# One-core decoder trunk: the first MLP product as seven block products, with weight sums in buffers of their own

## The chip, the cores and the metric

One NeuronCore of a Trainium2 chip runs the whole program. The time is the device time of one execution in microseconds (us); lower is better. TensorE (PE) multiplies, VectorE (DVE) and ScalarE (ACT) do elementwise work, GpSimd (POOL) issues the accumulating DMAs of this kernel, and SyncE (SP) issues the plain ones.

## The reference

A trunk of four layers over 512 tokens of 1024 features. Each layer adds a token mixer (sliding-window attention, a Conformer convolution, an HGRN2 recurrence, attention again) and then a squared-ReLU MLP with 4096 hidden features:

```python
def squared_relu_mlp(h, w1, w2):
    return jnp.square(jax.nn.relu(h @ w1)) @ w2
...
        h = h + y
        h = h + squared_relu_mlp(rms_norm(h, norm_mlp[i]), mlp_w1[i], mlp_w2[i])
    return rms_norm(h, final_norm)
```

All is float32. The factor of the norm is taken out of the MLP: the squared ReLU lets it be applied, squared, to the result (`r2`, `nr2`).

## The kernel before

**Precision.** Every operand is held as two float32r parts, high and low, and a product is three matmuls: high by high, high by low, low by high (lines 279 to 287). The high part is an ACT cast, the low part a DVE subtraction (`load`, line 262, for weights; line 557 and 558 for activations).

**Weights.** A plan lists all blocks of weights in the order of use, 512 KB each. `load` takes the next: a DMA into a `raw` tile on SP's queue, then the cast and the subtraction into a pair of tiles `wh`, `wl`, of which there are five (`W_BUFS`). `prefetch` runs it up to five blocks ahead of those that PE has finished (`n_done`), as the code is written out; each engine then works through its own list in order.

**The MLP** goes in four groups of 1024 hidden features a layer, 16 in all. The first product of a group is plain (`linear`): eight output tiles of 128 features, each 8 x 3 matmuls with 512 tokens as moving columns. The second product, 512 x 1024 by 1024 x 1024 in 2 x 2 blocks, is done with seven block products instead of eight (`PRODUCTS`). Each takes a block or a combination of blocks of the hidden activations U (s1 to s4) and of the weights W (t1 to t4):

```python
    ("U11 W11", "x", ((0, 0, 1),)),
    ("U12 W21", "z", ((0, 0, 1),)),
    ("s1 t1", "y", ((1, 1, -1),)),
    ("s2 t2", "x", ((0, 1, -1),)),
    ("s4 W22", "y", ((0, 1, -1),)),
    ("s3 t3", "x", ((1, 1, -1),)),
    ("U22 t4", "x", ((1, 0, 1),)),
```

The letter names a pair of PSUM banks that goes on accumulating; after the named product a result is read out and added to `rows` (line 604). A block of weights is 512 x 512 and comes in two halves, each one block of the plan (14 a group). t1, t2 and t4 are made one after the other in the tile that held W11, each by a DMA on POOL's queue that adds another block to the tile in place (line 217); t3 is made in the tile of W12 in that way. All these tiles come from a pool of the MLP with eight buffers (line 211), so each W block of a half has its own. Blocks of the first product use another pool, `rawp`, of three.

The s operands are made by DVE and cast by ACT up to three products ahead (`operand`). The normalised rows are turned by PE transposes into `xs`, 512 tokens wide, and PE starts on them as they come (`lead`).

## Time and profile before

| | us |
|---|---|
| median of 3 runs | 2170.0 (2169.82 to 2171.41) |
| the profiled execution | 2173.1, of which the span from first to last instruction is 2171.3 |
| PE busy | 2121.1 (98%) |
| PE weight loads, beside the matmuls | 1748.1 (81%) |
| DVE busy | 1402.4 (65%) |
| ACT busy | 1156.5 (53%) |
| POOL busy | 200.5 (9%) |
| mean DMA rate | 120 GB/s |

A busy PE is not a PE at its peak: matmuls overlap, and the records show each as longer than the step from one to the next. The granted clock of PE is full in nearly all of the span. Times of rows are from the start of the span. The waits of an engine that isn't the bottleneck cost nothing; those of PE do.

### The profile page before, as it was taken

Reading aid. Unit: us, or ns where it says so; the run is one execution under the profiler, and the core shown is the slowest. Engines: PE = TensorE matmul, PEld = TensorE weight load, DVE = VectorE, ACT = ScalarE, POOL = GpSimd, SP = SyncE. Lnnn points to the kernel's source line nnn. Section 1 sums busy time; section 2 is a strip of 40 time slices with the busy share of each in tenths; the row PEclk is TensorE's granted clock in tenths of the full one; section 3 lists DMA queues with packets and bytes.
Section 4 is the critical chain, followed back from the end, with each engine's and each line's share of the span. In section 5 each row is a group of like instructions: output and inputs, shape, how many; then the busy total and the mean of one; then the engine's idle time right before and its main releaser. Section 6 shows DMA issues by size and latency. Waiting matters only on the chain.

```text
span 2171.3 us, 27234 instructions
## 1 busy us (share of the span) xinstructions
PE 2121.1 (98%) x10226; PEld 1748.1 (81%) x10226; DVE 1402.4 (65%) x2226; ACT 1156.5 (53%) x2015; POOL 200.5 (9%) x193
## 2 busy tenths in 40 slices
PE   8999999999988999999999999999999999999997
PEld 7778888888877888888788888888887878888886
DVE  6864663769986375475888874547548784637547
ACT  6855454454684445445555554534536684534534
POOL 0000110110020011011300000101100000101100
PEclk9999999999998999999999999999999999999999
DMA  5154755745214375674222226567564116557553
GB/s 152 47 155 110 181 129 152 184 68 136 69 40 136 98 184 114 168 175 88 88 62 75 78 69 179 113 164 177 118 161 88 59 50 194 120 152 188 114 125 78
DMA packets 211063, 262.56 MB, mean 121 GB/s; under 512 B 9027, under 2 KB 136003, under 8 KB 210932
## 3 DMA queue, kind: packets, MB, share of 16 engines
q1 hardware_dynamic: 175540, 191.61, 28.1%
q0 software_dynamic: 35392, 69.21, 20.1%
q8 instruction: 81, 1.33, 0.2%
q14 instruction: 50, 0.41, 0.1%
HBM read 258.69 MB, written 2.10 MB: 120 GB/s over the span
## 4 chain that ended last, share of the span: by engine, by line
PE 72%; DVE 14%; ACT 5%; DMA 5%; issue 4%; SPq 0%; DVEq 0%; ACTq 0%
PE mm L285 21%; PE mm L286 21%; PE mm L287 21%; DVE wl L262 5%; DMA raw<-in_mlp_w_dram 4%; DVE rows L604 3%; PE aux L754 2%; DVE ul L558 2%; DVE uc L893 1%; PE aux L704 1%; ACT wh L262 1%; PE aux L1068 1%; ACT uc L912 1%; PE aux L438 1%; PE aux L738 1%
## 5 line engine op out<-in xcount | busy, mean ns | idle before, releaser
L262 DVE TENSOR_TENSOR wl<-raw,wh 128x1024 fp32r<-128x1024 f32 x452 | 551.2, 1220 | 538.9 <-ACT wh L262 536.3
L262 ACT CAST wh<-raw 128x1024 fp32r<-128x1024 f32 x452 | 470.0, 1048 | 497.7 <-PE mm L286 187.9
L285 PE MATMUL mm<-x,wh 128*128 128x512 f32 x1568 | 628.9, 401 | 0.0
L286 PE MATMUL mm<-x,wh 128*128 128x512 f32 x1568 | 613.7, 391 | 0.0
L287 PE MATMUL mm<-x,wl 128*128 128x512 f32 x1568 | 613.6, 391 | 0.0
L287 PEld LDWEIGHTS mm<-x,wl 128*128 128x128 f32 x1568 | 294.6, 188 | 62.5 <-issue 1.2
L286 PEld LDWEIGHTS mm<-x,wh 128*128 128x128 f32 x1568 | 295.6, 189 | 56.6 <-issue 1.8
L285 PEld LDWEIGHTS mm<-x,wh 128*128 128x128 f32 x1568 | 295.5, 188 | 55.7 <-issue 1.1
L285 PE MATMUL mm<-wh,uh 128*128 128x512 f32 x768 | 303.1, 395 | 15.9 <-DVE rows L604 12.6
L217 POOL DMA_DIRECT2D raw<-in_mlp_w_dram x128 | 153.5, 1206 | 1773.2 <-DVE wl L262 928.4
L286 PE MATMUL mm<-wl,uh 128*128 128x512 f32 x768 | 300.0, 391 | 0.0
L287 PE MATMUL mm<-wh,ul 128*128 128x512 f32 x768 | 298.0, 391 | 0.0
L285 PEld LDWEIGHTS mm<-wh,uh 128*128 128x128 f32 x768 | 144.5, 188 | 53.8 <-issue 10.6
L287 PEld LDWEIGHTS mm<-wh,ul 128*128 128x128 f32 x768 | 144.6, 188 | 30.3
L286 PEld LDWEIGHTS mm<-wl,uh 128*128 128x128 f32 x768 | 144.8, 189 | 28.9
L563 ACT ACTIVATE relu<-mm 128x512 f32<-128x512 f32 x128 | 76.0, 594 | 166.7 <-PE mm L287 166.7
L558 DVE TENSOR_TENSOR ul<-us,uh 128x1024 fp32r<-128x1024 f32 x64 | 78.0, 1218 | 32.5 <-ACT uh L557 32.5
L604 DVE SCALAR_TENSOR_TENSOR rows<-mm,nr,rows 128x512 f32<-128x512 f32 x128 | 94.9, 741 | 0.0
L564 ACT ACTIVATE us<-relu 128x512 f32<-128x512 f32 x128 | 80.9, 632 | 3.9
L285 PE MATMUL mm<-wh,y 128*128 128x512 f32 x192 | 78.1, 407 | 1.4 <-ACT y L366 1.4
L426 ACT ACTIVATE sq<-rows 128x512 f32<-128x512 f32 x64 | 40.2, 628 | 68.3 <-DVE rows L338 54.3
L287 PE MATMUL mm<-wh,y 128*128 128x512 f32 x192 | 76.0, 399 | 0.0
(232 smaller groups left out, 2546.5 us busy)
## 6 DMA issues: line engine op xcount, KB each, us to landing
raw<-in_mlp_w_dram SPq DMA_DIRECT2D x256, 512.0 KB
raw<-in_mlp_w_dram POOLq DMA_DIRECT2D x128, 512.0 KB, 6.1
raw<-in_hgrn_w_qfig_dram SPq DMA_DIRECT2D x64, 256.0 KB
raw<-in_attn_w_qkv_dram SPq DMA_DIRECT2D x20, 512.0 KB
raw<-in_attn_w_o_dram SPq DMA_DIRECT2D x16, 512.0 KB
raw<-in_conv_w_pw_dram SPq DMA_DIRECT2D x32, 256.0 KB
raw<-in_conv_w_pw_dram SPq DMA_DIRECT2D x8, 512.0 KB
raw<-in_hgrn_w_o_dram SPq DMA_DIRECT2D x8, 512.0 KB
```

The costliest lines, as they stand in the source:

```text
L217: gp.dma_start(out=wide(to), in_=block(w, r, c, h), accum_op=ALU.add)
L262: return sc.copy(wh, raw), ve.tensor_tensor(wl, raw, wh.bitcast(F32), ALU.subtract)
L285: pe.matmul(ps, sh, mh, start=start, stop=False, skip_group_check=again)
L286: pe.matmul(ps, sh, ml, start=False, stop=False, skip_group_check=again)
L287: pe.matmul(ps, sl, mh, start=False, stop=stop, skip_group_check=again)
L426: sc.activation(scratch("sq"), rows[:, b, f * T : (f + 1) * T], AF.Square, accum_out=self.ms[:, f, b : b + 1])
L438: pe.transpose(ps[:, b * P : (b + 1) * P], rows[:, b, j * P : (j + 1) * P], ident)
L558: ve.tensor_tensor(flat[1], src, flat[0].bitcast(F32), ALU.subtract)
L563: sc.activation(s, ps, AF.Relu)
L564: sc.activation(us[j // KH][:, :, j % KH, :], s.rearrange("p (h t) -> p h t", h=2), AF.Square)
L604: ve.scalar_tensor_tensor(o, banks[bank][p], norm.r2[sign][:, b : b + 1], o, ALU.mult, ALU.add)
L754: pe.matmul(po[h * HD : (h + 1) * HD, n * P : (n + 1) * P], vtok[:, n - 1 + b, kv * HD : (kv + 1) * HD], pT[:, b, n - n0, h, :], start=b = ...
```

## The change

The first product now goes through the same seven block products. Its roles are swapped against the second one: weight blocks of 128 x 128 are stationary, and the normalised activations, cut into halves of 256 tokens, move. So PE issues 7 x 2 x 2 x 4 x 3 = 336 matmuls of 256 columns a group instead of 192 of 512, and the plan has 28 blocks a group instead of 22. `BlockNorm` turns the rows into `xf`, unsplit, and `Operands` makes the x operands once a layer and the u operands once a group. t2 of the first product is added on DVE (`on_chip`), the other combinations of both products by DMA.

Only the tiles that hold W11, t1, t2 and t4 stay in the MLP's pool, now of four buffers (two halves of two products). W21, W22 and W12 (with t3) of both products go through `rawp` with its three buffers. In both products the last two of the seven are done one PSUM bank after the other. The u operands get their own room, and two accumulators of the convolution move to another pool.

```diff
...
         for g in range(FF // D):
-            add_cols([[(mlp_w1[i], D * g + SLAB * s, SLAB)] for s in range(4)], (0, 1))
-            add_products(mlp_w2[i][D * g : D * (g + 1), :])
+            add_products(mlp_w1[i][:, D * g : D * (g + 1)], ("t2",))
+            add_products(mlp_w2[i][D * g : D * (g + 1), :], ())
...
-    def summed(w, group, name, h):
-
-
-        def get(r, c):
+    def summed(w, group, name, h, on_chip):
+
+
+        def get(r, c, pool=rawp, **k):
             key = (r, c, h)
             if key not in group:
-                group[key] = raw_tile(sumpool[0], bufs=8)
+                group[key] = raw_tile(pool, **k)
                 nc.sync.dma_start(out=wide(group[key]), in_=block(w, r, c, h))
             return group[key]
 
         def add(to, r, c):
-            if SUMS_BY_DMA:
+            if name in on_chip:
+                ve.tensor_tensor(to, to, get(r, c), ALU.add)
+            else:
                 gp.dma_start(out=wide(to), in_=block(w, r, c, h), accum_op=ALU.add)
-            else:
-                ve.tensor_tensor(to, to, get(r, c), ALU.add)
             return to
 
         if name == "11":
+            if sumpool[0]:
+                group["sum", h] = get(0, 0, sumpool[0], bufs=4)
+                return group["sum", h]
             return get(0, 0)
         if name == "21":
             return get(1, 0)
         if name == "22":
             return get(1, 1)
         if name == "t1":
-            return add(get(0, 0), 0, 1)
+            if ("sum", h) not in group:
+
+                del group[0, 0, h]
+                group["sum", h] = get(0, 0, sumpool[0], bufs=4)
+            return add(group["sum", h], 0, 1)
         if name == "t2":
-            return add(get(0, 0), 1, 1)
+            return add(group["sum", h], 1, 1)
         if name == "t3":
             return add(get(0, 1), 1, 1)
-        return add(get(0, 0), 1, 0)
+        return add(group["sum", h], 1, 0)
 
...
     def prefetch():
         i = len(loaded)
-        if i < len(plan) and i - n_done < W_BUFS and not (plan[i][0] == "sum" and sumpool[0] is None):
+        if i < len(plan) and i - n_done < W_BUFS and not (plan[i][0] == "sum" and plan[i][3] not in ("11", "21") and sumpool[0] is None):
...
+    class BlockNorm(Norm):
+
+
+        def __init__(self, key, i):
+            super().__init__(key, i)
+            self.xf = {}
+            self.turned = [False, False]
+
+        def turns(self, f):
+            yield 2
+            H = T // 2
+            self.xf[f] = [xcp.tile([P, KH, H], F32, tag="xc", name="xf") for _ in range(2)]
+            for j in range(f * KH, (f + 1) * KH):
+                ps = self.turn(j)
+                for t in range(2):
+                    sc.activation(self.xf[f][t][:, j % KH, :], ps[:, t * H : (t + 1) * H], AF.Copy, scale=vec(self.key, j, self.i))
+                yield 1
+            self.turned[f] = True
+
     class Last:
 
 
...
+    class Operands:
+
+
+        def __init__(self, block, room, chain):
+            self.block, self.room, self.chain, self.ops = block, room, chain, {}
+            self.sums = None
+        def make(self, name):
+            if name in self.ops:
+                return
+            what = name.split()[0]
+            if what == "s1":
...
+            else:
+                src = self.block(int(what[2]) - 1, int(what[1]) - 1)
+            hi, lo = self.room()
+            flat = [t.rearrange("p k t -> p (k t)") for t in (hi, lo)]
+            sc.copy(flat[0], src)
+            ve.tensor_tensor(flat[1], src, flat[0].bitcast(F32), ALU.subtract)
+            self.ops[name] = hi, lo
...
+            def room_u():
+                rooms[0] += 1
+                if rooms[0] % U_BUFS == 0:
+                    return [xcp.tile([P, KH, H], F32R, tag="xc", name=n) for n in ("uh", "ul")]
+                u = mp.tile([P, 2, KH, H], F32R, tag="u", name="u", bufs=U_BUFS - 1)
+                return u[:, 0], u[:, 1]
+
+            X = Operands(lambda h, t: flat(norm.xf[h][t]), room_x, chain)
...
-                def hidden(j, ps):
-                    s = scratch("relu")
-                    sc.activation(s, ps, AF.Relu)
-                    sc.activation(us[j // KH][:, :, j % KH, :], s.rearrange("p (h t) -> p h t", h=2), AF.Square)
-                    if j == KH - 1:
-                        operand(PRODUCTS[0][0])
-
-                linear(norm.xs, 4, hidden, lead=KC - 1 if g == 0 else None)
-
+                U = Operands(lambda h, t: flat(us[h][:, t]), room_u, chain)
+
+
+                banks, begun = {}, set()
+                for q, (name, bank, reads) in enumerate(PRODUCTS):
+                    while not all(norm.turned[: 1 if q == 0 else 2]):
+                        pump()
+                    X.make(name)
+                    fresh = bank not in banks
+                    if fresh:
+                        banks[bank] = [ps_aux() if bank == "z" else ps_main() for _ in range(2)]
+                    hi, lo = X.ops[name]
+                    u0 = take(2)
+
...
+                    in_turn = q >= len(PRODUCTS) - 2
+                    for ms in ((0, 1), (2, 3)) if in_turn else (range(KH),):
+                        for h in range(2):
+                            for k in range(2):
+                                wh, wl = (wide(w)[:, k, :] for w in unit(u0 + h))
+                                for m in ms:
+                                    c = slice(m * P, (m + 1) * P)
+                                    begins = fresh and h == 0 and k == 0
+                                    step(
+                                        banks[bank][m // 2][:, m % 2 * H : (m % 2 + 1) * H], (wh[:, c], wl[:, c]),
+                                        (hi[:, 2 * h + k, :], lo[:, 2 * h + k, :]),
+                                        begins and m % 2 == 0, h == 1 and k == 1, True, begins,
+                                    )
+                                    if h == 1 and k == 1 and m % 2:
+                                        evac(m // 2)
+                            if KH - 1 in ms and not in_turn:
+                                n_done += 1
+                            if h == 0 and ms[0] == 0 and q + 1 < len(PRODUCTS) and all(norm.turned):
+                                X.make(PRODUCTS[q + 1][0])
+                            if h == 0 and ms[0] == 0 and q + 1 == len(PRODUCTS):
+                                U.make(PRODUCTS[0][0])
+                    if in_turn:
+                        n_done += 2
...
-                    ends = last and q == len(PRODUCTS) - 1
+                    in_turn = q >= len(PRODUCTS) - 2
...
-                    if ends:
+                    if in_turn:
                         for p in range(2):
                             for h in range(2):
                                 one(p, h)
-                            evac(p)
+                            add(p)
                         n_done += 2
                     else:
                         for h in range(2):
                             for p in range(2):
                                 one(p, h)
                                 if h == 1:
-                                    evac(p)
+                                    add(p)
                             n_done += 1
             sumpool[0] = None
...
```

In the three pieces of instruction order below, tiles carry numbers. First SP's queue for the second product of the third group of the first layer. Before, `raw_3142` and `raw_3187` are the two halves of W11, `raw_3210` and `raw_3255` of W21, `raw_3370` and `raw_3389` of W22, `raw_3413` and `raw_3433` of W12:

```order
L212 DMA raw_3142<-in_mlp_w2_dram 128x2x512
L212 DMA raw_3187<-in_mlp_w2_dram 128x2x512
L212 DMA raw_3210<-in_mlp_w2_dram 128x2x512
L212 DMA raw_3255<-in_mlp_w2_dram 128x2x512
L212 DMA raw_3370<-in_mlp_w2_dram 128x2x512
L212 DMA raw_3389<-in_mlp_w2_dram 128x2x512
L212 DMA raw_3413<-in_mlp_w2_dram 128x2x512
L212 DMA raw_3433<-in_mlp_w2_dram 128x2x512
```

And now, for the same group, W21 is `raw_3781` and `raw_3837`, W22 `raw_3937` and `raw_3960`, W12 `raw_3979` and `raw_4003`; the waits of each are shown:

```order
L212 DMA raw_3781<-in_mlp_w2_dram 128x2x512 [waits DMAHW2_49,DVE_49]
L212 DMA raw_3837<-in_mlp_w2_dram 128x2x512 [waits DMASW6_49,DVE_49]
L212 DMA raw_3937<-in_mlp_w2_dram 128x2x512 [waits DMASW1_49,DVE_49]
L212 DMA raw_4059<-in_mlp_w1_dram 128x2x512 [waits DMAHW0_49,DMASW7_49,DVE_49]
L212 DMA raw_4078<-in_mlp_w1_dram 128x2x512 [waits DMAHW1_49,DMASW0_49,DVE_49]
L212 DMA raw_3960<-in_mlp_w2_dram 128x2x512 [waits DMAHW5_49,DVE_49]
L212 DMA raw_3979<-in_mlp_w2_dram 128x2x512 [waits DMAHW6_49,DMAHW3_49,DVE_49]
L212 DMA raw_4003<-in_mlp_w2_dram 128x2x512 [waits DMAHW7_49,DMAHW4_49,DVE_49]
L212 DMA raw_4097<-in_mlp_w1_dram 128x2x512 [waits DMAHW5_49,DVE_49,Activation_49]
```

Eight loads in a row, of which each found a buffer of its own, have become a chain through three buffers: `raw_4003`, the last one, takes the buffer of `raw_3937` and waits for DVE to have split that.

POOL's queue of accumulating DMAs for that product, before: the two halves of t3 (`raw_3413`, `raw_3433`) ahead of all, then t1, t2 and t4 in the tiles of W11.

```order
L217 DMA raw_3413<-in_mlp_w2_dram 128x2x512
L217 DMA raw_3433<-in_mlp_w2_dram 128x2x512
L217 DMA raw_3142<-in_mlp_w2_dram 128x2x512
L217 DMA raw_3187<-in_mlp_w2_dram 128x2x512
L217 DMA raw_3142<-in_mlp_w2_dram 128x2x512
L217 DMA raw_3187<-in_mlp_w2_dram 128x2x512
L217 DMA raw_3142<-in_mlp_w2_dram 128x2x512
L217 DMA raw_3187<-in_mlp_w2_dram 128x2x512
```

Now, with `raw_3699` and `raw_3759` as the tiles of W11:

```order
L219 DMA raw_3699<-in_mlp_w2_dram 128x2x512
L219 DMA raw_3759<-in_mlp_w2_dram 128x2x512
L219 DMA raw_3699<-in_mlp_w2_dram 128x2x512
L219 DMA raw_3979<-in_mlp_w2_dram 128x2x512
L219 DMA raw_3759<-in_mlp_w2_dram 128x2x512
L219 DMA raw_3699<-in_mlp_w2_dram 128x2x512
L219 DMA raw_3759<-in_mlp_w2_dram 128x2x512
L219 DMA raw_4003<-in_mlp_w2_dram 128x2x512
```

The two of t3 (`raw_3979`, `raw_4003`) have moved from the head of the list into its middle and end: the first half between the two halves of t2, the second half behind t4.

DVE at the start of the second product, before, from the split of the first half of t1 (`wl_3290`) to that of the second half of W22 (`wl_3392`); `ul_` rows make low halves of operands, L543 is s1, L546 s2, L552 s3, L549 s4:

```order
L262 TENSOR_TENSOR wl_3290<-raw_3142,wh_3289 128x1024
L558 TENSOR_TENSOR ul_3268<-us_2990,uh_3267 128x1024
L543 TENSOR_TENSOR us_sum_3271<-us_2990,us_2989 128x1024
L604 SCALAR_TENSOR_TENSOR rows_89<-mm_3277,r2_1893,rows_89 128x512
L262 TENSOR_TENSOR wl_3308<-raw_3187,wh_3307 128x1024
L558 TENSOR_TENSOR ul_3274<-us_sum_3271,uh_3273 128x1024
L604 SCALAR_TENSOR_TENSOR rows_89<-mm_3278,r2_1893,rows_89 128x512
L546 SCALAR_TENSOR_TENSOR us_sum_3271<-us_sum_3271,us_2989 128x1024
L262 TENSOR_TENSOR wl_3331<-raw_3142,wh_3330 128x1024
```

Now, with L554 for s1, L563 s3, L557 s2; `wl_3840` is the second half of W21, `wl_3858` the first of t1, `wl_3881` the second, `wl_3898` the first of t2:

```order
L269 TENSOR_TENSOR wl_3840<-raw_3837,wh_3839 128x1024
L269 TENSOR_TENSOR wl_3858<-raw_3699,wh_3857 128x1024
L554 TENSOR_TENSOR sum_3821<-us_3363,us_3362 128x1024
L563 TENSOR_TENSOR us_3362<-us_3362 128x1024
L700 SCALAR_TENSOR_TENSOR rows_89<-mm_3826,r2_1899,rows_89 128x512
L569 TENSOR_TENSOR u_3823<-sum_3821,u_3823 128x1024
L700 SCALAR_TENSOR_TENSOR rows_89<-mm_3827,r2_1899,rows_89 128x512
L557 SCALAR_TENSOR_TENSOR sum_3821<-sum_3821,us_3362 128x1024
L269 TENSOR_TENSOR wl_3881<-raw_3759,wh_3880 128x1024
L269 TENSOR_TENSOR wl_3898<-raw_3699,wh_3897 128x1024
```

The second half of t1 had three instructions between it and the first half; it now has six.

## Rows read from the trace of the kernel before

**Rows 1.** The page, its first part: busy time of each engine, share, instructions.
```profile
PE 2121.1 (98%) x10226; PEld 1748.1 (81%) x10226; DVE 1402.4 (65%) x2226; ACT 1156.5 (53%) x2015; POOL 200.5 (9%) x193
```

**Rows 2.** Stretches, first and second product: PE, PEld, DVE, ACT, POOL, clock, DMA share, GB/s.
```profile
250.70:294.00 43.30, 43.30 (x192) 35.86 (x191) 12.45 (x11) 17.54 (x23) 2.38 (x2) 1.00 0.55 134
294.20:333.20 39.00, 38.31 (x169) 31.40 (x169) 34.00 (x35) 21.33 (x22) 7.15 (x6) 1.00 0.73 175
```

**Rows 3.** Timeline of PE among attention scores: start us, duration, instruction.
```profile
125.50 0.28 PE L704 MATMUL aux<-kh,qs 128*128 128x256 f32 x1
125.62 0.28 PE L704 MATMUL aux<-kl,qs 128*128 128x256 f32 x1
125.75 0.40 PE L286 MATMUL mm<-wl,y 128*128 128x512 f32 x1
125.98 0.39 PE L287 MATMUL mm<-wh,y 128*128 128x512 f32 x1
```

**Rows 4.** Waits of PE: us in total, times, longest.
```profile
PE mm L285 <- DVE rows L604: 12.6, 16, 1.5
```

**Rows 5.** Groups by line: busy us, mean ns, idle before, and what ended it.
```profile
L262 DVE TENSOR_TENSOR wl<-raw,wh 128x1024 fp32r<-128x1024 f32 x452 | 551.2, 1220 | 538.9 <-ACT wh L262 536.3
L262 ACT CAST wh<-raw 128x1024 fp32r<-128x1024 f32 x452 | 470.0, 1048 | 497.7 <-PE mm L286 187.9 <-DMA raw<-in_mlp_w_dram 181.2 <-PE mm L287 113.6
```

**Rows 6.** Stretches with one accumulating DMA, one plain DMA, another plain one.
```profile
285.70:288.30 2.60, 2.60 (x13) 2.17 (x12) 0.00 (x0) 0.00 (x0) 0.00 (x0) 1.00 1.02 172
288.50:290.50 2.00, 2.00 (x11) 1.65 (x10) 0.00 (x0) 1.23 (x2) 0.00 (x0) 1.00 0.72 266
294.90:297.00 2.10, 2.10 (x11) 1.72 (x10) 1.23 (x1) 2.04 (x4) 0.17 (x1) 1.00 0.75 244
```

**Rows 7.** Timeline of SP's queue: first issue at, merged with the next ones.
```profile
285.68 8.53 SPq L212 DMA_DIRECT2D raw<-in_mlp_w_dram  x2
...
334.07 5.58 SPq L251 DMA_DIRECT2D raw<-in_mlp_w_dram  x2
```

**Rows 8.** Timeline of ACT: start us, duration, instruction, wait before and its end.
```profile
308.19 2.94 ACT L262 CAST wh<-raw 128x1024 fp32r<-128x1024 f32 x3 [2.48 <-DMA raw<-in_mlp_w_dram]
...
336.94 1.05 ACT L262 CAST wh<-raw 128x1024 fp32r<-128x1024 f32 x1 [4.59 <-DMA raw<-in_mlp_w_dram]
```

**Rows 9.** The page, its last part: accumulating DMAs, KB each, us to landing.
```profile
raw<-in_mlp_w_dram POOLq DMA_DIRECT2D x128, 512.0 KB, 6.1
```

**Rows 10.** Timeline of POOL in the second product.
```profile
302.00 1.20 POOL L217 DMA_DIRECT2D raw<-in_mlp_w_dram  x1 [3.99 <-DVE wl L262]
```

**Rows 11.** Timeline of DVE in the second product, which starts at 294.25.
```profile
298.69 1.22 DVE L543 TENSOR_TENSOR us_sum<-us 128x1024 f32<-128x1024 f32 x1
299.82 0.74 DVE L604 SCALAR_TENSOR_TENSOR rows<-mm,r,rows 128x512 f32<-128x512 f32 x1
300.48 1.22 DVE L262 TENSOR_TENSOR wl<-raw,wh 128x1024 fp32r<-128x1024 f32 x1
...
309.27 1.23 DVE L262 TENSOR_TENSOR wl<-raw,wh 128x1024 fp32r<-128x1024 f32 x1 [1.23 <-ACT wh L262]
...
311.55 1.22 DVE L262 TENSOR_TENSOR wl<-raw,wh 128x1024 fp32r<-128x1024 f32 x1
```

**Rows 12.** Stretches around a stop of PE in the convolution.
```profile
630.40:634.80 4.40, 0.30 (x3) 0.11 (x1) 4.40 (x4) 3.12 (x8) 2.28 (x2) 1.00 0.22 84
634.90:639.60 4.70, 0.00 (x0) 0.00 (x0) 4.49 (x7) 4.57 (x12) 0.00 (x0) 0.50 0.36 112
639.70:645.10 5.40, 5.40 (x22) 4.54 (x22) 0.75 (x2) 4.46 (x12) 0.00 (x0) 0.50 0.01 3
645.20:651.40 6.20, 6.20 (x50) 5.61 (x50) 6.02 (x6) 5.27 (x13) 3.31 (x2) 1.00 0.00 0
```

**Rows 13.** Timeline of PE at the lower clock.
```profile
671.29 0.63 PE L287 MATMUL mm<-wh,z 128*128 128x512 f32 x1
671.71 0.63 PE L285 MATMUL mm<-wh,z 128*128 128x512 f32 x1
```

More of the change, by code (lines that the diff above doesn't have):

```diff
@@ L34 @@
 U_BUFS = 3
-SUMS_BY_DMA = True
 PRODUCTS = (
@@ L164, in add_products @@
             for h in range(2):
-                plan.append(("sum", w, group, WEIGHT_OF[name], h))
+                plan.append(("sum", w, group, WEIGHT_OF[name], h, on_chip))
     def attn_slabs(i):
@@ L277, in take, with step @@
         return n_taken - n
-    def step(ps, st, mv, start, stop, again=False):
+    def step(ps, st, mv, start, stop, again=False, pin=False):
         nonlocal n_steps
         (sh, sl), (mh, ml) = st, mv
-        pe.matmul(ps, sh, mh, start=start, stop=False, skip_group_check=again)
-        pe.matmul(ps, sh, ml, start=False, stop=False, skip_group_check=again)
-        pe.matmul(ps, sl, mh, start=False, stop=stop, skip_group_check=again)
+        parts = (sh, mh), (sh, ml), (sl, mh)
+        for n, (a, b) in enumerate(parts):
+            ins = pe.matmul(ps, a, b, start=start and n == 0, stop=stop and n == 2, skip_group_check=again)
+            if pin and n == 0:
+                keep(ins)
         if n_steps % KH == KH - 2:
@@ L511, in block @@
             nc.sync.dma_start(out=out[0, b * P : (b + 1) * P, :], in_=row)
+    class Operands:
[7 more added lines that the diff above has]
+            if what == "s1":
+                src = self.sums = self.chain()
+                ve.tensor_tensor(src, self.block(1, 1), self.block(0, 1), ALU.subtract)
+            elif what == "s2":
+                src = self.sums
+                ve.scalar_tensor_tensor(src, src, -1.0, self.block(0, 0), ALU.mult, ALU.subtract)
+            elif what == "s4":
+                src = self.sums
+                ve.scalar_tensor_tensor(src, src, -1.0, self.block(1, 0), ALU.mult, ALU.subtract)
+            elif what == "s3":
+                src = self.block(0, 1)
+                ve.tensor_tensor(src, self.block(0, 0), src, ALU.subtract)
+            else:
[5 more added lines that the diff above has]
+            self.ops[name] = hi, lo
     def mlp(i, norm, nxt):
@@ L523, in mlp, with flat, chain, room_x @@
             H = T // 2
+            def flat(t):
+                return t.rearrange("p k t -> p (k t)")
+            def chain():
+                return mp.tile([P, KH * H], F32, tag="sum", name="sum")
+            def room_x():
+                return [xcp.tile([P, KH, H], F32R, tag="xc", name=n) for n in ("xh", "xl")]
+            rooms = [0]
+            def room_u():
[4 more added lines that the diff above has]
+                return u[:, 0], u[:, 1]
@@ L525, in mlp @@
+            X = Operands(lambda h, t: flat(norm.xf[h][t]), room_x, chain)
             alone = []
             for g in range(groups):
+                last = g == groups - 1
                 us = [mp.tile([P, 2, KH, H], F32, tag="us", name="us", bufs=2) for _ in range(2)]
-                U11, U21, U12, U22 = (us[h][:, t].rearrange("p k t -> p (k t)") for h in range(2) for t in range(2))
-                sums, ops = {}, {}
-                def chain():
-                    if "s" not in sums:
-                        sums["s"] = xcp.tile([P, KH * H], F32, tag="xc", name="us_sum")
-                    return sums["s"]
@@ L570, in mlp @@
+                if last and nxt is None:
+                    nxt = Last(mp)
                 banks = {}
-                last = g == groups - 1
                 for q, (name, bank, reads) in enumerate(PRODUCTS):
                     for n, _, _ in PRODUCTS[q : q + U_BUFS]:
-                        operand(n)
+                        U.make(n)
                     fresh = bank not in banks
@@ L1231, in trunk_kernel @@
     for i in range(DEPTH):
-        mid = Norm("norm_mlp", i)
+        mid = BlockNorm("norm_mlp", i)
         if i % 3 == 0:
```

48 lines of the change are left out of this document (19 added, 29 removed).

## The prediction

> **What bounds the kernel now.** I read the page first: PE is busy 98% of the span and DVE 65% [rows 1]. Then the stretches of one feed-forward group: the first product is 43.3 us in which PE never stops, 192 matmuls, so 226 ns each; the second is 39.0 us with 169, and there DVE is busy 34 us (87%) against 12 to 13 us in the first [rows 2]. So PE sets the pace, and weights are made ready with little to spare in the second product only. Sixteen such groups are about 1320 us of the 2171. The profiled execution took 2173.1 us, 3 above the median of 2170.0; I sum against 2173 and take 3 off at the end.
>
> **First product: what it gives.** 192 matmuls of 512 columns become 336 of 256 (7 products, 2 halves, 2 x 4 tiles, 3 terms), each with its own weight load. Their price is in the trace: in a run of attention scores two 128x256 matmuls and a following one start 0.12 and 0.13 us apart, against 0.23 us for 512 columns [rows 3]. 336 x 0.12 = 40.3 us, so 3.0 us less a group, 48 us in all. Bounds: at 0.116 (half of 0.23) 39.0, at 0.13 43.7, so -69 to +6 us; I take 0.12, since the operand types and the alternation of weight load and matmul are those of that row. A bank at a time for the last two products removes a wait of PE for `rows` between the sixth and seventh, 12.6 us in 16 waits [rows 4]: -13.
>
> **What it adds in weights.** 28 blocks of 512 KB a group are split instead of 22, each an ACT cast of 1.05 and a DVE difference of 1.22 us [rows 5]. DVE in the first product then has 14 x 1.22 + 2 x 1.22 (t2 on the chip) + 6 additions of some 0.7 + one operand = 25 us of 40: hidden. In the first group of a layer seven x operands join (7 x 1.22 and 4 combinations of the same size, 13.4 us): 38 of 40, with each combination needing 3.5 us (difference, cast, difference) where half a product lasts 2.9. I put 2.3 us of waits there (0 to 8): +9 us for four layers. PSUM evacuation on ACT and DVE fits in the same way.
>
> Of DMA there are 14 accumulating transfers a group instead of 8, beside 16 plain ones as before. One accumulating transfer keeps the 16 engines at a share of 1.02 while it runs, from 285.1 to 288.7 or 3.6 us as I read it; a plain one costs 1.6 (0.75 of 2.1 us) [rows 6]. 14 x 3.6 + 16 x 1.6 = 76 us of a group of about 79: no room to catch up once something is late.
>
> **Second product: what it costs.** Its arithmetic stays, 168 x 0.227 = 38.1 us. What changes is where its blocks lie while they wait. Before, all had eight buffers of their own: W22 and W12 came a group ahead, and both accumulations into t3 were done during the product before. Now they go through the ring of three that the first product uses as well. I call the 14 blocks 11a, 11b, 21a ... t4b; PE needs block n at 2.72 n us (12 x 0.227) after the start T.
>
> The ring decides this: 21a, 21b, 22a, 22b, 01a, 01b in turn, so 01b (the base of t3b) can't be loaded before 22a is split, and then comes a load, an accumulation and a split, in a row. Between the first use of 22a and of t3b lie 2 x 2.72 + 6 x 0.227 = 6.8 us, since the sixth product now runs a bank at a time and wants its second block after six matmuls. The chain: 0.2 to issue; a load 2.9 (issued at 334.07, cast begins at 336.94) [rows 7, 8]; the accumulation 6.1 [rows 9]; cast and difference 2.3: 11.5 us. So PE waits 4.7 us less the time by which 22a is ahead.
>
> Is 22a ahead? Before, T was 294.25. t1b was split at 301.70 (T+7.5), its accumulation t2b was issued at 302.00, and the cast of t2b waited for it until 308.19 (T+13.9) [rows 8, 10, 11]; t2b was ready at T+16.3 and 22a at T+18.5, 3.3 us ahead of T+21.8 [rows 11]. After, the last product of the first MLP product runs a bank at a time, so it holds its two blocks to T; 21b and t1a are both cast only from T: 21b ready at 2.3, t1a at 3.4. Then DVE has, in its order, s1 (which waits for ACT's last square at 3.3), s3, rows, s1's low half, rows, s2 and only then t1b. From start to start 1.14 us for a 1024-wide one and 0.66 for rows [rows 11]: t1b from 9.2 to 10.4. Accumulation of t2b: 16.8, and 17.3 with t3a's ahead of it on POOL. Cast and difference: 19.7, against 19.05 wanted. On ACT s4's cast and on DVE its low half and a `rows` stand before 22a: 22.6, against 22.5 wanted by then. So 22a has no lead left, PE has waited 0.8, and t3b costs 4.7; with t4b's accumulation (issued at 19.9, engines full until 25.5) ahead of the load, 1.7 us more: a plain load issued at 285.68 came through only from 288.5, at 266 GB/s, when an accumulation had left the engines [rows 6, 7]. So 4.7 to 6.7; with the lead of before 1.4 less at the low end after its own knock-on, 3.3; with the next group's loads of 21a and 21b beside it (2 us), 8. I take 0.8 + 6.0, nearest to the full chain.
>
> A page of the Trainium skill would make this chain shorter: DMA: Bandwidth & Descriptors, section on the anatomy of one SWDGE transfer, gives 2.0 us plus bytes over 436 GB/s, an estimate of 3.2 us for 512 KB. The chain holds two such transfers (t2b, t3b), so by the page the wait would nearly vanish. The trace has 6.1 [rows 9], and that decides.
>
> PE standing still also costs clock. PE was idle from 630.7 to 639.7: the granted share was 0.50 (1.2 of 2.4 GHz) from 634.9, stayed there for 5.4 us after matmuls came back, and was 1.00 from 645.2 [rows 12]. A 512-column matmul then takes 0.42 instead of 0.23 [rows 13]: up to 5.4 x (1 - 0.23/0.42) = 2.5 us a stop. There it fell after PE had stood still for 4.2 us; a stop of 6 us is longer. 0 to 2.5, I take 2.0.
>
> A stop repeats in each group: the lead at T is set by the five split buffers, not by the group before. First product after it: its t3b chain is the same length, but t2 needs no transfer there, so 22a is split three blocks ahead and t3b is ready at about the moment it is wanted (28 to 30 us against 30.0): 0 to 1.5, I take 0.
>
> **Sum.** 2173 - 48 - 13 + 9 + 16 x (0.8 + 6.0 + 2.0 = 8.8) = 2173 - 52 + 141 = 2262, less 3: 2260 us. Ends of this case: 16 x 4.1 = 66 without loss of clock and without the first-group waits gives 2175; 16 x 11.5 = 184 (8 + 1 + 2.5) with 32 for the first groups gives 2325.
>
> **Rivals.** *Faster: the supply holds.* If t3b's load and accumulation are done by T+27 (22a split by T+16, because t1b is split as early as before and loads pass accumulations), PE never stops: 2173 - 52 - 3 = 2118. For it: before, the wait for t2b stayed hidden, with 2.7 us to spare (T+16.3 against T+19.0). Against it: 11.5 us of chain in 6.8 us. It turns at a wait of 3.3 us a group: 16 x 3.3 = 52; below that the change gains. *In between:* waits of 1 to 4 us, too short for the clock to fall: 2118 + 16 to 64 = 2134 to 2182. *The products don't get cheaper, so that the change misses its aim:* if a weight load can't run beside the matmul before it, a 256-column step takes about the 0.227 of a 512-column one, and the first product 76 us instead of 43: above 2600. The starts of 0.12 us, each with its own load, speak against it [rows 3]; the Trainium skill (TensorE: Matmul & The Clock Gate, part 3 on packing small matmuls) has loads overlap only where row groups differ, which that row contradicts.
>
> **How the numbers follow.** A measurement here tells about 0.2% (4 us) from no change. The stop at t3b as summed: 0.67, 2175 to 2325, likeliest 2260. In between: 0.15, half of it below 2166. Supply holds: 0.14, 2110 to 2134. Slower than 2325 (weight loads, longer queues): 0.04. Faster then has 0.14 + 0.07 = 0.21, same 0.04, slower 0.75. The range from 2135 to 2325 leaves out the case that supply holds and the slow tail, 0.18; both signs are in it, and the likeliest case's own range is 2175 to 2325.
>
> **What would show it.** Right: the first product of a later group at 40 to 41 us with matmuls 0.12 us apart; one PE wait of 4 to 8 us in each second product, before the second block of its sixth product, ended by DVE's `wl`, that by ACT's cast, that by a transfer of POOL's queue; and a share of 0.5 in the clock behind it. Wrong: second products of 39 us; a load of 01b that goes out before 22a is split; accumulations of 4 us; the 256-column matmuls at 0.13 or more; or the waits in the first product instead.

## The result: 2327.5 us, slower by 7.2%, and the profile after

The changed kernel takes 2327.5 us (median; 2325.7 to 2328.2) against 2170.7 before: a ratio of 1.072, 95% interval 1.0706 to 1.0733. The forecast was 2260 in a range of 2135 to 2325, so the direction was right, the size 67 us short, and the time lies 2.5 us above the range.

The page of the changed kernel, its busy line and its accumulating DMAs (columns as in [rows 1] and [rows 9]):

```profile
span 2324.0 us, 32907 instructions
PE 2133.5 (92%) x12530; PEld 1842.1 (79%) x12530; DVE 1643.6 (71%) x2462; ACT 1310.8 (56%) x2267; POOL 316.4 (14%) x289
...
raw<-in_mlp_w_dram POOLq DMA_DIRECT2D x224, 512.0 KB, 6.2
```

PE is busy for 12 us more than before, but its share falls from 98% [rows 1] to 92%: about 190 us of the span PE now stands still. The stretches of one feed-forward group, first and second product (duration, PE busy, clock, DMA share, GB/s), beside [rows 2]:

```profile
262.40:306.05 43.65, 41.13 (x338) 1.00 0.72 167
306.05:355.40 49.35, 41.69 (x171) 0.93 0.79 171
```

Neither is cheaper. I summed all 16 groups from the start of the first matmul of each product: the first products took 703.6 us before and 714.4 after, the second ones 640.3 and 783.5. That is 154 us, nearly all of the loss; the stages outside the MLPs hardly moved.

The 256-column matmuls themselves cost what the forecast said. In a first product (timeline of PE: start, duration) they start 0.12 us apart, each with its own weight load (the page counts as many loads, 12530, as matmuls):

```profile
300.84 0.28 PE L294 MATMUL mm<-xh,wl 128*128 128x256 f32 x1
300.96 0.28 PE L294 MATMUL mm<-xh,wh 128*128 128x256 f32 x1
301.08 0.28 PE L294 MATMUL mm<-xl,wh 128*128 128x256 f32 x1
301.20 0.28 PE L294 MATMUL mm<-xh,wl 128*128 128x256 f32 x1
```

So 336 x 0.12 = 40.3 of the 43.65 us is work. The rest, and the 10 us of the second product, are waits. The waits of PE over the span (us in total, times, longest), where [rows 4] stood before:

```profile
PE mm L294 <- ACT wh L269: 103.2, 16, 7.6
PE mm L294 <- DVE us L636: 30.1, 31, 2.4
PE mm L294 <- ACT us L631: 11.4, 12, 1.7
PE mm L294 <- DVE wl L269: 7.6, 17, 0.5
```

The first and the last are the second products: 16 stops, one in each. The two between them are the first products. The wait for `rows` of [rows 4] is gone.

One stop, followed through the engines (timelines of DVE, SP's queue, POOL, ACT and PE in the second product that starts at T = 306.06; start, duration, idle time before and what ended it):

```profile
327.31 1.22 DVE L269 TENSOR_TENSOR wl<-raw,wh 128x1024 fp32r<-128x1024 f32 x1
...
328.55 0.37 SPq L212 DMA_DIRECT2D raw<-in_mlp_w_dram  x1
...
325.90 1.19 POOL L219 DMA_DIRECT2D raw<-in_mlp_w_dram  x1 [6.69 <-DVE wl L269]
333.73 1.20 POOL L219 DMA_DIRECT2D raw<-in_mlp_w_dram  x1 [6.65 <-DVE wl L269]
...
341.79 3.89 ACT L269 CAST wh<-raw 128x1024 fp32r<-128x1024 f32 x4 [11.76 <-DMA raw<-in_mlp_w_dram]
...
335.31 0.39 PE L294 MATMUL mm<-wh,u 128*128 128x512 f32 x1
342.89 0.80 PE L294 MATMUL mm<-wh,u 128*128 128x512 f32 x1 [7.20 <-ACT wh L269]
344.15 0.80 PE L294 MATMUL mm<-wl,u 128*128 128x512 f32 x1 [0.46 <-DVE wl L269]
```

The reader is to see the chain of the prediction, link by link. 22a is split at 328.53 (T+22.5). At 328.55 the slot is free and SP issues the load of 01b. At 333.73, 5.2 us later, POOL can issue the accumulation that makes t3b of it. At 341.79, 8.1 us after that, ACT's cast begins, having waited 11.76 us for a DMA; the three casts merged with it stood behind it in ACT's order and followed at once. PE had run out at 335.5 and goes on when the cast is done. The matmul before the stop is the 126th of 168: 5 x 24 + 6, just ahead of the second block of the sixth product.

The clock behind this stop (stretches of PE: duration, busy, granted clock, DMA share, GB/s), to be read like [rows 12]:

```profile
339.00:340.70 1.70, 0.00 (x0) 1.00 0.88 160
340.70:342.80 2.10, 0.00 (x0) 0.51 0.06 10
344.10:346.00 1.90, 1.85 (x4) 0.50 0.47 78
347.50:349.50 2.00, 2.00 (x10) 0.98 1.01 371
```

The granted share fell to 0.50 (1.2 of 2.4 GHz) at about 340.8, when PE had stood still for 5 us, and was back at 347.5. The pattern is the same in all 16 groups: a step of 5.8 to 8.0 us at this matmul, 6.8 on average, where 0.23 is normal.

In the first product PE stops at places that the forecast had put at nothing. Timeline of DVE at the end of that first product, which started at 262.5:

```profile
299.74 1.23 DVE L569 TENSOR_TENSOR ul<-us,uh 128x1024 fp32r<-128x1024 f32 x1 [1.08 <-ACT uh L568]
301.21 1.23 DVE L269 TENSOR_TENSOR wl<-raw,wh 128x1024 fp32r<-128x1024 f32 x1 [0.25 <-ACT wh L269]
302.35 0.68 DVE L636 TENSOR_TENSOR us<-us,mm 128x512 f32<-128x512 f32 x1
```

The addition at 302.35 empties the bank of PSUM that the second half of the seventh product is to write. PE had finished that bank at 298.15. The addition stands in DVE's order behind the low half of an operand and a `wl`, and each of these waited for its cast on ACT. PE waits for it behind its 312th matmul: a step of 1.53 us where 0.12 is normal, after 0.83 behind the 288th (the other bank) and 0.99 behind the 240th. The stop behind the 240th is ended by ACT, whose copy out of PSUM stands behind the cast of a block that came late (timeline of ACT):

```profile
290.55 1.05 ACT L269 CAST wh<-raw 128x1024 fp32r<-128x1024 f32 x1 [9.20 <-DMA raw<-in_mlp_w_dram]
291.51 0.58 ACT L631 COPY us<-mm 128x512 f32<-128x512 f32 x1
```

### The profile page after: what moved, and what is told of

Its sections match the earlier page's. It is cut to its first block, busy times and chain, and to the rows that moved or that the text cites. A ratio compares the mean times of both kernels' runs of the same rounds, so it can differ in the third digit from the quotient of the medians.

```text
span 2324.0 us, 32907 instructions
## 1 busy us (share of the span) xinstructions
PE 2133.5 (92%) x12530; PEld 1842.1 (79%) x12530; DVE 1643.6 (71%) x2462; ACT 1310.8 (56%) x2267; POOL 316.4 (14%) x289
## 4 chain that ended last, share of the span: by engine, by line
PE 47%; DMA 22%; DVE 13%; ACT 10%; issue 6%; POOL 1%; SPq 0%; POOLq 0%; ACTq 0%; DVEq 0%
PE mm L294 36%; DMA raw<-in_mlp_w_dram 21%; DVE wl L269 5%; ACT wh L269 5%; PE aux L294 4%; PE aux L850 2%; DVE uc L989 1%; ACT us L637 1%; PE aux L800 1%; DVE rows L700 1%; PE aux L1164 1%; ACT uc L1008 1%; DVE us L636 1%; PE aux L447 1%; DVE u L569 1%
## 5 line engine op out<-in xcount | busy, mean ns | idle before, releaser
L294 PE MATMUL mm<-xh,wh 128*128 128x256 f32 x1536 | 439.8, 287 | 41.7 <-DVE us L636 30.1
L294 PE MATMUL mm<-xl,wh 128*128 128x256 f32 x1536 | 434.9, 283 | 4.6 <-DVE xl L569 4.6
L294 PE MATMUL mm<-xh,wl 128*128 128x256 f32 x1536 | 434.2, 283 | 0.3 <-DVE wl L269 0.3
L294 PE MATMUL mm<-wh,u 128*128 128x512 f32 x1024 | 346.5, 410 | 52.2 <-ACT wh L269 51.4
L294 PE MATMUL mm<-x,wh 128*128 128x512 f32 x1088 | 358.5, 408 | 0.0
L294 PEld LDWEIGHTS mm<-xh,wh 128*128 128x128 f32 x1536 | 294.1, 192 | 52.1 <-DVE us L636 30.3
L294 PEld LDWEIGHTS mm<-xl,wh 128*128 128x128 f32 x1536 | 294.4, 192 | 6.7 <-DVE xl L569 6.0
L294 PEld LDWEIGHTS mm<-xh,wl 128*128 128x128 f32 x1536 | 294.3, 192 | 0.5 <-DVE wl L269 0.5
L294 PEld LDWEIGHTS mm<-x,wh 128*128 128x128 f32 x1088 | 193.9, 189 | 33.9 <-issue 2.9
L294 PE MATMUL mm<-x,wl 128*128 128x512 f32 x544 | 214.6, 395 | 0.0
```

Source lines behind the costliest of these rows:

```text
L294: ins = pe.matmul(ps, a, b, start=start and n == 0, stop=stop and n == 2, skip_group_check=again)
```

## The experiments: is it the ring, and why does the gain not arrive?

My theory: the ring of three `rawp` buffers makes the stop, since 01b cannot be loaded before 22a is split, and the waits in the first product are its after-effect. Rivals: the DMA engines simply have too much to carry (224 accumulating transfers in place of 128); or the order on DVE is the cause, which the planner (the scheduler that places the instructions on each engine when the kernel is built) chooses anew with each change.

**A ring of four.** Four buffers do not fit beside the rest, so room is taken from the scratch pool of the other stages:

```
-    rawp = ...tc.tile_pool(name="rawp", bufs=3)
+    rawp = ...tc.tile_pool(name="rawp", bufs=4)
-    tmp = ...tc.tile_pool(name="tmp", bufs=6)
+    tmp = ...tc.tile_pool(name="tmp", bufs=4)
```

> The changed kernel with a ring of four buffers in place of three (room for it comes from the scratch pool of the other stages, six buffers to four). Theory (the ring): 01b, the base of t3b, takes the slot that 21b leaves some 20 us earlier, so that only the accumulation of 6.1 us and the split of 2.3 us could be late, and they start early. The stop of 5.8 to 8.0 us before matmul 126 of each second product vanishes, and with it the time at half clock behind it: second products go from 49 to about 40 us, 16 x 9 = 144 us off 2327, so about 2180 (2165 to 2200). Rival (the 16 DMA engines have too much to carry, with 14 accumulating transfers a group): the loads only start earlier and share the same engines, a stop of 4 us or more stays at the same place or moves to another block, and the time is above 2270.

Its control, with the scratch pool alone cut:

> Control for the run with a ring of four: the changed kernel with the scratch pool of the other stages cut from six buffers to four and nothing else. Both theories: 2327, within 5 us, if four buffers are enough for those stages; what it is above that has to be added to the gain of the ring of four.

Measured: 2165.7 us with the ring of four (ratio to before 0.9977, 0.9967 to 0.9986), and 2334.1 with the smaller scratch pool alone (one run). So one more buffer is worth 168 us, and the smaller pool costs about 7, as far as one run can tell. Stretches of one group with the ring of four, first and second product:

```profile
333.30:373.60 40.30, 40.30 (x338) 1.00 0.82 189
373.60:414.40 40.80, 39.29 (x171) 1.00 0.88 200
```

The first product is at exactly 40.3 us, with no wait at all, in all 12 groups that are not the first of a layer. The engines carry the same bytes in less time (200 GB/s in place of 171), so that they had too much to carry is refuted. In the timelines of SP's queue and POOL of that second product, T = 373.6,

```profile
374.55 0.37 SPq L212 DMA_DIRECT2D raw<-in_mlp_w_dram  x1
...
377.56 2.90 POOL L219 DMA_DIRECT2D raw<-in_mlp_w_dram  x2
```

the last load for this second product goes out at T+0.95, not at T+22.5, and with it the accumulation for t3b, the last of three that POOL issues in a row, at T+5.3 (the second in the row shown, merged with the one at T+4); with the ring of three it went out at T+27.7. The theory's size was right (2180 expected, 2165 to 2200). What is left over are steps of 1 to 2 us at other places: behind PE's 144th matmul (1.6 to 1.7 us in 15 groups) and behind the 85th (the second block of t2, up to 1.3 us in 15 groups).

**The ring by itself, in the kernel before.** The second product's W21, W22 and W12 go through the ring; all else stays:

```
-                group[key] = raw_tile(sumpool[0], bufs=8)
+                group[key] = raw_tile(sumpool[0], bufs=4) if key[:2] == (0, 0) else raw_tile(rawp)
```

> The kernel before with one part of the change alone: the blocks W21, W22 and W12 of the second product go through the ring of three, W11 and its sums keep buffers of their own, four. First products, the order of blocks and the number of accumulations stay as before. Theory (ring and lead together): 22a is split at T+18.5 as before, the chain of 11.5 us ends at T+30 to 31.7, and with blocks by halves PE wants t3b only at T+29.9: stops of 0 to 2 us a group and no loss of clock, 2171 to 2205. If the ring alone makes the stop: 6 to 7 us and a half clock of 7 to 10 us behind it in each group, 2290 to 2330. If the ring has no part in it: 2171.

> The kernel before with the second product's blocks through a ring of four (scratch pool six to four for room); with a ring of three it took 2283. Theory (the ring alone): 01b takes 21b's slot and the stop before t3b goes: 2171 to 2185. Rival (that all blocks come at most a ring ahead and share it with the next group's loads is what costs, whatever the number): 2220 or above.

Measured: 2283.0 with a ring of three (ratio 1.0519, 1.0503 to 1.0535), 2185.2 with a ring of four and the smaller scratch pool (1.0065, 1.0048 to 1.0081). A second product of each (three, then four):

```profile
391.50:438.00 46.50, 41.48 (x169) 0.93 0.69 152
...
376.70:416.60 39.90, 38.42 (x170) 1.00 0.80 175
```

So the ring of three is worth 112 us with the old first products and the old order of blocks, and the fourth buffer gives back 98. The 15 us that are left lie in the second products, mainly at short waits behind the 102nd and the 144th matmul. My own expectation of 0 to 2 us a group was wrong: PE stops 4.1 to 5.3 us in 14 of 16 groups. 22a is ready when I said, at T+18.8, but what follows is longer (timelines of SP's queue, POOL and ACT, ring of three in the kernel before, T = 391.5):

```profile
410.30 0.37 SPq L212 DMA_DIRECT2D raw<-in_mlp_w_dram  x1
...
416.43 1.20 POOL L217 DMA_DIRECT2D raw<-in_mlp_w_dram  x1 [6.94 <-DVE wl L262]
...
424.60 2.94 ACT L262 CAST wh<-raw 128x1024 fp32r<-128x1024 f32 x3 [11.53 <-DMA raw<-in_mlp_w_dram]
```

The load takes 6.1 us until POOL goes on and the accumulation 8.2 until the cast begins, 14.3 in place of the 9.2 (0.2 + 2.9 + 6.1) that I had put there.

**One accumulation less in the chain.** t2 of the second product is added on DVE, from the W22 block that is in the ring anyway:

```
-            add_products(mlp_w2[i][D * g : D * (g + 1), :], ())
+            add_products(mlp_w2[i][D * g : D * (g + 1), :], ("t2",))
```

> The changed kernel with t2 of the second product added on DVE from the W22 block in the ring, as the first product does, in place of an accumulating transfer. The ring stays at three. Theory (a chain in a row): the accumulation of 6.1 us between t1b's split (T+9.9) and t2b's cast (T+17.2) goes, one addition of about 1.2 us comes; t2b is split at about T+14 in place of 19.5, 22a at about T+17 in place of 22.4, and t3b's load, accumulation and split of 11.5 to 15 us end at T+29 to T+32 where PE wants it at 27 to 28: the stop shrinks from 6.9 to 1 to 4 us and the clock holds in most groups, so 16 x (4 to 9) = 64 to 144 us less, 2185 to 2265. Rival (the DMA engines have too much to carry): 12 accumulations a group in place of 14 is a seventh less, the stop shrinks by 1 us at most, and the time is above 2300. Second rival (DVE is the limit in the second product): two additions more on DVE make the splits later, and the time is 2327 or above.

Measured: 2300.6 (ratio 1.060, 1.0584 to 1.0616), so 27 us less than the changed kernel, and above the theory's 2185 to 2265. 22a is split at T+19.5, 3 us earlier than before, not 5, and the chain behind it is the same (T = 398.8; POOL's issue for t3b at T+24.8):

```profile
423.56 1.20 POOL L219 DMA_DIRECT2D raw<-in_mlp_w_dram  x1 [6.64 <-DVE wl L269]
```

The cast begins at T+32.8, 8.0 us later, and PE still stops 4.5 to 5.6 us in 15 groups (6.3 in the last); in all 16 the granted clock fell to 0.50 behind the stop. Partly right: the lead of 22a matters, but only by what it shortens the stop, 1.7 us on average, and 16 x 1.7 is the 27 us. The first rival's time, above 2300, is just met, but it allowed the stop to shrink by 1 us at most.

**What the chain is made of.** The two accumulations of t4 in each second product are left out:

```
-        return add(group["sum", h], 1, 0)
+        return add(group["sum", h], 1, 0) if on_chip else group["sum", h]
```

> The changed kernel, ring of three, with the two accumulating transfers of t4 in each second product left out, so that t4 is t2 there and the sum lacks W21. The question is what the 15 us from 22a's split to t3b's cast are made of (load 5.2, accumulation 8.1 as traced, 2.9 and 6.1 in the prediction). Theory (transfers beside it): without t4's accumulations ahead of it the load takes about 3 us, the accumulation 6 to 8, and the stop before t3b falls from 6.9 to 3 to 5 us, with the clock held in some groups: 2327 - 16 x (2 to 6) = 2230 to 2295. Rival (each transfer is that long by itself here): the stop stays at 6 to 7 us, 2315 or above.

Measured: 2311.7 (one run), between the theory and the rival and nearer to the rival. The stop is 6.1 us on average in place of 6.8. Timelines of POOL and ACT in a second product (T = 305.7):

```profile
331.79 1.20 POOL L219 DMA_DIRECT2D raw<-in_mlp_w_dram  x1 [14.44 <-DVE rows L700]
...
340.71 3.89 ACT L269 CAST wh<-raw 128x1024 fp32r<-128x1024 f32 x4 [11.40 <-DMA raw<-in_mlp_w_dram]
```

Without t4's accumulations ahead of it the load takes 4.1 us instead of 5.3 until POOL goes on (means of the 16 groups), but the accumulation still takes 8.1 (8.9 in this group), against 7.7 in the changed kernel. What may stretch it is seen in the last group of the changed kernel, behind which no loads for a next group follow (timelines of POOL and ACT):

```profile
2297.01 1.20 POOL L219 DMA_DIRECT2D raw<-in_mlp_w_dram  x1 [6.84 <-DVE rows L700]
...
2302.88 1.04 ACT L269 CAST wh<-raw 128x1024 fp32r<-128x1024 f32 x1 [10.43 <-DMA raw<-in_mlp_w_dram]
```

There it is 5.9 us. In the other 15 groups SP issues plain loads of 1 MB in all for the next group or layer, mostly two of 512 KB, from 3.4 us before POOL issues the accumulation to 0.4 us after it, and the accumulation takes 7.1 to 8.4. In three groups of the run with t2 on DVE the first of these loads went out 4.4 to 4.7 us ahead, and there it took 5.7 to 6.2. That these loads are the cause fits the four traces with a ring of three that I looked at, but it is not shown: no run was made with the loads alone held back.

**Order on DVE.** The ring of four, with the differences on DVE kept in the order in which the program writes them:

```
+        if sumpool[0]:
+            keep(both[1])
...
-            ve.tensor_tensor(flat[1], src, flat[0].bitcast(F32), ALU.subtract)
+            keep(ve.tensor_tensor(flat[1], src, flat[0].bitcast(F32), ALU.subtract))
```

> The ring of four, and on DVE the differences (wl) of the weights and of the operands keep the order in which the program writes them, so that none of them is run ahead of an addition to rows. In the run with the ring of four PE still stopped 1.25 us before matmul 144, the first of the seventh product, while DVE ran two wl of 1.22 us ahead of the addition of 0.74 us that frees the bank of PSUM. Theory (order on DVE): that wait goes, 16 x 1.25 = 20 us less than 2166: 2146 (2135 to 2158). Rival (DVE is short of time, not of order): the two wl come later then and PE waits for them in place of the bank: 2160 to 2185.

The same with t2 on DVE, and then with the ring set back to three:

> The run before this (ring of four, order on DVE kept) with t2 of the second product added on DVE from the W22 block, in place of the accumulating transfer. With the ring of four PE stopped 0.9 to 1.3 us before the second block of t2 in about ten groups, and it was its cast that came late, behind the transfer. Theory (chain through t2b): that stop goes too, and 12 accumulations in place of 14 leave the engines freer: 10 to 18 us less than the run without it, about 2130 (2118 to 2140). Rival (DVE is the limit in the second product, 34 of 39 us busy before, now 2 x 1.22 us more): splits come late elsewhere, 2150 or above.

> The kernel that ran in 2141 (ring of four, order of the differences on DVE kept, t2 on DVE) with the ring set back to three and nothing else. It asks whether the number of buffers is the cause or the order on DVE, which the planner also chose anew when the ring grew. Theory (the ring): the stop before t3b is back in each group, 4.7 + 1.3 us and half clock behind it as in the run with t2 on DVE alone, so 2141 + 16 x 8 = 2270 (2245 to 2310). Rival (the order): with the order kept the time stays within 15 us of 2141.

Measured: 2189.4, 2140.6 and 2342.1. The first refutes my forecast of a gain: kept order costs 24 us. The wait before the seventh product goes, but PE waits for casts instead, most of all for that of t2b (waits of PE over the span):

```profile
PE mm L297 <- ACT wh L269: 32.4, 33, 2.8
```

The third settles ring against order: with the differences kept in the same order and POOL's program the same, three buffers in place of four cost 202 us, more than the 104 to 169 that I had expected (the additions may still stand elsewhere among the differences). Its stretches, first and second product of one group:

```profile
260.00:303.60 43.60, 40.90 (x338) 1.00 0.74 173
303.60:352.50 48.90, 41.76 (x169) 0.93 0.64 147
```

The stop in the second product is back, and so are the 3.3 us in the first, where the ring of four has none with either order. So the first product's waits come with the ring too: blocks that arrive late are split late, and the work that empties PSUM stands behind them.

**Ring of four and t2 on DVE, order left to the planner.**

> The ring of four with t2 of the second product on DVE, the order on DVE left to the planner. It tells which of the two steps gave the 25 us from 2166 to 2141. Theory (t2b's transfer): the stop of about 1 us before t2b's block goes, the wait of 1.25 us before the seventh product stays: 2150 to 2158. Rival (only both together help, since kept order alone made 2189): 2162 or above.

Measured: 2120.1 us (ratio to before 0.9768, 0.9753 to 0.9782), below both expectations and the best kernel of this study. Page, and one group's stretches:

```profile
PE 2079.6 (98%) x12530; PEld 1819.6 (86%) x12530; DVE 1681.5 (79%) x2494; ACT 1324.8 (63%) x2267; POOL 277.0 (13%) x257
...
326.70:367.10 40.40, 40.40 (x338) 1.00 0.80 186
367.10:405.90 38.80, 38.80 (x171) 1.00 0.81 186
```

PE does not wait once in either product of this group, and the wait for `rows` before the seventh product is gone with that for t2b. That it was an after-effect, DVE catching up after the late block, is my reading and not shown: with the ring of four alone it stood also in groups in which PE had not waited for t2b. t2 on DVE gave 27 us with the ring of three, 46 with four.

**A bank at a time.** With the ring of four, the last two products go block by block again, in the second and then in the first product:

```
-                    in_turn = q >= len(PRODUCTS) - 2
+                    in_turn = last and q == len(PRODUCTS) - 1
...
-                    in_turn = q >= len(PRODUCTS) - 2
+                    in_turn = False
```

> The ring of four with the last two products of the second MLP product block by block again, as in the kernel before (but for the last product of a layer): what is a bank at a time worth by itself? By the prediction it saves the wait of PE for rows between the sixth and the seventh product, 13 us in all: then 2166 + 13 = 2179. Theory from the run with the ring of four: that wait is there with a bank at a time too (1.25 us before matmul 144), so nothing is lost without it: 2155 to 2170.

> The ring of four with the first product's last two products block by block in place of a bank at a time; the rest as changed. What is that part worth there? The prediction put the emptying of PSUM in the first product at 0 to 1.5 us a group. Theory (as in the second product, where block by block cost 33 us in 16 groups): PE waits 1 to 2.5 us before the seventh product for the bank that an addition on DVE frees: 2180 to 2205. Rival (the first product has room on DVE): 2160 to 2172.

Measured: 2199.3 (34 us more than the 2165.7 of the ring of four) and 2182.9 (17 more). So with a ring of four this part of the change gains, in both places, more than I gave it. In the second product (timelines of DVE and PE without it):

```profile
1520.60 3.48 DVE L269 TENSOR_TENSOR wl<-raw,wh 128x1024 fp32r<-128x1024 f32 x3
1524.00 1.40 DVE L700 SCALAR_TENSOR_TENSOR rows<-mm,nr,rows 128x512 f32<-128x512 f32 x2
...
1524.88 0.76 PE L294 MATMUL mm<-wh,u 128*128 128x512 f32 x1 [2.91 <-DVE rows L700]
```

both banks come due at once and DVE empties them behind three `wl`; PE waits 2.9 us where it waited 0.8 on average before (12.6 us in 16 [rows 4]), and behind this stop the granted clock fell to 0.50 in 12 of the 16 groups. In the first product the time came out as my theory said and the mechanism did not: the first product is only 0.45 us longer, 40.8 instead of 40.3,

```profile
250.90:291.70 40.80, 40.80 (x339) 1.00 0.85 202
291.70:334.10 42.40, 39.26 (x168) 1.00 0.84 180
```

7 us in all, and the second products are 6 us longer, with waits behind the 72nd matmul for the low half of an operand (`DVE u L569`, 13.5 us in 12 over the span). The other 4 of the 17 us are no loss of this run: the profiled execution of the ring of four took 2172.05 us, 6 more than its median, so that the two traces are only 12 us apart.

## Why the prediction was wrong in size, step by step

**256-column matmuls at 0.12 us: right.** 40.3 us is the whole first product wherever PE did not wait (five of the six runs with a ring of four in the changed kernel, later groups of a layer); the rival that a weight load cannot run beside the matmul before it fell at once.

**First product "0 to 1.5, I take 0": the step that failed.** The sum had 703.6 - 48 + 9 = 665 us for the 16 first products; they took 714. These 50 us are most of the 67 that were missing. I had followed t3b's chain in the first product, given it 0 to 1.5 us and taken the lower end, and had let "PSUM evacuation on ACT and DVE fits in the same way" stand on DVE's busy share (25 of 40 us). It was 25.9 of 43.7, so that was right, and proved nothing: the additions, and ACT's copies out of PSUM, stand in one queue with splits that wait for late blocks. Three stops of about 1, 0.8 and 1.5 us follow. They make 3.3 us a group (43.6 in place of 40.3, mean of the 12 later groups), and one buffer more took them away. The range's upper end left out even the 16 x 1.5 = 24 us that the text itself named; with it, 2327.5 would have lain inside.

**First groups: 9 us forecast, 13 measured** with the ring of four (43.7 against 40.3 us in three layers, 43.0 in the other).

**Second product: 141 - 13 = 128 us forecast, 143.2 measured; near, by terms that partly cancel.** The place and the clock are as forecast, and the releasers but for the last: ACT's cast, not DVE's `wl`, lets PE go on. Its terms: no wait at t2b or 22a (0.8 forecast), since 22a was ready at T+22.5, as I had it; the stop 6.8 less one step of 0.23 = 6.6 (6.0 forecast) and 0.5 more for `wl`; clock 2.2 in the group shown (2.0), summed over the ten steps behind the stop, each less 0.23 and less the 0.5. Inside the stop, two links were short. I took 0.2 + 2.9 for the load and up to 1.7 for t4b's accumulation ahead of it; 4.8 together, and the mean is 5.3. I took 6.1 for the accumulation, the median of the profile's page [rows 9]; in this place it takes 7.7 on average, probably because the next group's loads run beside it, as the last group suggests. The bound of 8 us in the text had that; it belonged into the value. At the end I had counted 2.3 us for cast and difference; PE goes on after the cast, 1.05, and then waits 0.5 for the difference. The Trainium skill (DMA: Bandwidth & Descriptors, the section on the anatomy of one SWDGE transfer) would have made the wait nearly vanish, with an estimate of 3.2 us by its formula for such a transfer; the trace decides against it, with 7.7 us.

**A bank at a time, -13 us: right in sign.** The wait of [rows 4] is gone. Leaving this part out cost 34 us in the second product and 17 in the first, with a ring of four; with three it was not tried.

**Rival "the supply holds", 2118 us: refuted for this kernel; its number came out in another.** With one more buffer and t2 added on DVE the supply does hold, and the time is 2120.1: 2118 plus about 7 for the smaller scratch pool is 5 us above it.

**Rival "in between": it counted on the clock to hold behind waits of 1 to 4 us.** The runs show less room: block by block, waits of 2.6 to 3.05 us were followed by a granted clock of 0.50 in 12 groups.

## What to carry to other kernels

When buffers of their own become a shared ring, write down for each block which earlier block must be finished before its load can go out; a chain of load, accumulation and split that fits in no gap costs its excess in every round, and one buffer more can be worth more than the change itself (168 us here; with t2 on DVE as well the kernel ends 50 us below the one before). Late blocks cost twice: once where PE waits for them, and again where other work stands behind their splits in an engine's queue, so an engine that is busy 60% of the time is not thereby free when it is wanted. Price a transfer by the rows of the moment in which it will run, with what else is in flight then, not by the median of the span.

## What the runs showed of the hardware

- An accumulating DMA of 512 KB took 5.9 us from issue to the cast that waits for it when no other load was issued near it (last group of the changed kernel), and 7.1 to 8.4 us in the 15 groups where plain loads of 1 MB in all were issued from 3.4 us before it to 0.4 us after it.
- Behind stops of 4.5 to 6.3 us (t2 on DVE, ring of three) the granted clock fell to 0.50 in all 16 groups, behind waits of 2.4 to 3.05 us (ring of four, second product block by block) in 12 of 16, and behind waits of 1.2 to 1.3 us (ring of four) in none of 15.
- Over the span the changed kernel spent 156 us at half clock, 126 of them in its 16 groups; the kernel before 37, of which 3 in its groups. At 512 columns the matmuls started 0.43 us apart at half clock, against 0.23.
